# Two sets of seven products without a use, behind the last router product and in front of the part with further rows

## The chip, the cores and the metric

The kernel runs on one core of a Trainium2 chip. The metric is device time in microseconds (us) from the start of the launch to its end. Times of single instructions, waits and granted clocks come from one profiled execution of the kernel before. TensorE is written PE, VectorE DVE, ScalarE ACT, GpSimd POOL and SyncE SP, as the profile writes them.

## What is computed

One layer of an encoder on 2048 tokens (rows) of width 1024: a token mixer, then a hierarchical mixture of experts with a gated embedding per layer.

```python
h1 = layernorm(x)                              # and the mixer: in-projection, conv and pooling groups, out-projection
x1 = layernorm(ALPHA * x + mixer(h1))
g  = softmax(x1 @ w_rg + b_rg); group = argmax(g)              # 4 groups
e  = x1 @ w_re + b_re, only the 8 experts of that group
top2 = top_k(e, 2); weight = softmax(top2) * g[group]
y  = sum over the 2 experts of  weight * ((silu(x1 @ w1) * (x1 @ w3)) @ w2)
ple = sigmoid(x1 @ w_pg + b_pg) * (p @ w_pp)
out = layernorm(ALPHA * x1 + y + ple)
```

Rows are sorted by expert into blocks of 128 slots. A fixed number of slots is planned for each expert; rows beyond that go through a loop over further blocks, whose length is read from the router's result at run time.

## The kernel before

**Products.** Almost every matrix product is made of three products of split operands (`mm3`, L222 to L224): a value is written as a high part (ACT, L356) and the rest (DVE or POOL, L357, `split`), so each weight tile costs one ACT and one DVE or POOL instruction of 128x1024 ahead of its products. A weight comes over SP's DMA queue (L1132) into a raw buffer (RB or RY) and is split into FB. PSUM has eight banks (PS), handed out by `SP = Slots(8)`, the one that has been free longest first; `take` and `get` fetch a bank, `free` gives it back.

**Stages.** First come the mixer's projections for 16 tiles of 128 rows. The out-projection leaves x1 tile by tile; each tile is normalised and turned by PE transposes (`transpose8`, L363). `router(c)` (L883, L884) makes the 36 router logits of the chunk of four tiles c, 16 products of 128x512; `logits` (L890, L891, L898, L899) adds bias, turns and stores them, and `route` (DVE, from L945 on) finds group, two experts and weights of each row. After the last chunk, c = 3, the counts over all rows are made (L1006, L1026, L1024, L1019, L1023 on PE, L1012 to L1070 on DVE), and the slots: DVE builds one-hot tables (L1080, L1082, L1089), PE multiplies them (L1094, 32 products of 128x40 in f32, each of two records in the trace) and the row numbers TBI and TBH (L1099, L1100) start the gathers of the experts' rows (L1387 on POOL's queue).

While that runs, the embedding part works for some of the tiles, PRE (`embed`): products with `w_pg` (L222 to L224), then for each tile L1280 (DVE), a tanh (L1282, ACT), the product with `w_pp`, L1286 and L1290 (DVE), and `base_done` writes the rows to the DRAM tensor `based` (L1321, POOL's queue). Then come the experts, with their first products L1574 and their second ones in `stage2`.

**Where the change touches it.** `run(router(3))` (L1376) makes the last router products; the jobs of the list `bg` are stepped between them. Later, behind the calls of `need` for the first experts' rows, `nc.values_load(novi)` (L1705) reads the number of further blocks on every engine and `tc.For_i` (L1707) loops over them; nothing moves across this loop. The rows of this input need no further block: the trace has no instruction of the loop's body.

**What sets the order.** The text of the program is not the order in which an engine gets its instructions. A scheduler reorders them inside a stretch between branches by its own estimate of times, and PSUM banks and buffers are given out as the program is written. Two instructions are held in order by `add_manual_dep(..., NoSync)`, which adds no wait on the chip. An engine runs its own instructions in the order set, and an instruction that waits holds back those behind it on the same engine.

At L391 and L431 the kernel already has products of the unit matrix `ident` by itself, at its start.

Of the kernel before, what the change touches and what calls it, by code (L numbers as in the profile page):

```python
# [183 lines left out]
def hybrid_conv_pool_hmoe_encoder(ctx, tc, x, p, ln0_g, ln0_b, w_in, b_in, conv_w, pool_w, pool_scale,  # L184
                                  w_o, ln1_g, ln1_b, w_rg, b_rg, w_re, b_re, w1, w3, w2, w_pg, b_pg,
                                  w_pp, ln2_g, ln2_b, out):
    nc = tc.nc
# [10 lines left out]
    PS = psum.tile([128, 8, 512], F32, name="PS")  # L198
    SF, SR, SZ, SP = Slots(NF, NY), Slots(NR), Slots(NZ), Slots(8)
# [30 lines left out]
    ident = consts.tile([128, 128], F32, name="ident")  # L230
# [62 lines left out]
    @contextmanager  # L293
    def behind(last):

        block = nc.cur_bb.bb
        n = len(block.instructions)
        yield
        for ins in list(block.instructions)[n:]:
            if ins.engine in last and ins.engine != mybir.EngineType.SP:  # L300
                tc.add_manual_dep(ins, last[ins.engine].name,
                                  mybir.DependencyInfo(mybir.DependencyClass.NoSync, mybir.DependencyReason.DATA),
                                  reason="in order")

    bg = Background()
    turn = [0]
# [5 lines left out]
    def run(gen):  # L312
        for _ in gen:
            bg.step()
# [8 lines left out]
    def start(name, gen, rate):  # L323
        jobs[name] = gen
        bg.add(gen, rate)

    def need(name):

        if name in jobs:
            gen = jobs.pop(name)  # L330
            n = 0
            while next(gen, DONE) is not DONE:
                n += 1
                if n > 40:
                    bg.step()
            bg.forget(gen)
# [401 lines left out]
    for s, j, c in units:  # L738
# [27 lines left out]
        with behind(beginning if (s, j, c) == (0, 0, 0) else {}):  # L766
            run(unit(s, j, c))
# [60 lines left out]
    def chunk_views(c):  # L828
        h, l = x1T[c]
        return [FB[:, q:q + 4].rearrange("p a (k t) -> p (a k) t", t=CH) for q in (h, l)]  # L830
# [48 lines left out]
    def router(c):  # L879
        vh, vl = chunk_views(c)  # L880
        b = SP.get()
        for k in range(KD):
            nc.tensor.matmul(PS[:, b], wrhv[:, k], vh[:, k], start=k == 0, stop=False)  # L883
            nc.tensor.matmul(PS[:, b], wrlv[:, k], vl[:, k], start=False, stop=k == KD - 1)  # L884
            yield
        start(f"logits{c}", logits(c, b), 1.0)

    def logits(c, b):
        z = SZ.get()
        nc.scalar.activation(ZB[0:36, z, :CH], PS[64:100, b], AF.Identity, bias=brc[0:36])  # L890
        nc.vector.tensor_add(ZB[0:36, z, :CH], ZB[0:36, z, :CH], PS[0:36, b])  # L891
        SP.free(b)
        yield
        yield
        b = SP.get()
        pv = PS[:, b, :4 * 36].rearrange("p (t e) -> p t e", e=36)
        for q in range(4):
            nc.tensor.transpose(pv[:, q], ZB[0:36, z, q * 128:(q + 1) * 128], ident[0:36, 0:36])  # L898
        nc.scalar.copy(LG[:, 4 * c:4 * c + 4], pv)  # L899
        SP.free(b)  # L900
        SZ.free(z)
        yield
# [271 lines left out]
    def take(slots, m=1, align=1):  # L1174
        n = 0
        while not slots.has(m, align):
            bg.step()
            n += 1
            assert n < 10000, "no slot"
        return slots.get(m, align)  # L1180
# [193 lines left out]
    SR.free(g1)  # L1374
    SR.free(b1)
    run(router(3))  # L1376
    SF.free(wrh)
    SF.free(wrl)
    for q in range(3):
# [320 lines left out]
    for m in members[ORDER[0]]:  # L1700
        need(f"g{m}")


    others, bg.jobs = bg.jobs, []
    nov_n = nc.values_load(novi[0:1, 0:1], min_val=0, max_val=NOV)  # L1705
    nc.vector.memset(ctr, 0.0)
    with tc.For_i(0, nov_n, 1) as it:  # L1707
# [5 lines left out]
        b = SP.get()  # L1713
# [146 lines left out]
    def gate_end(z, o, cols):  # L1860
# [3 lines left out]
        return v  # L1864

    def stage(i, t, ahead, behind):

        if i % 2 == 0 and 6 <= i + 4 < len(END):
# [72 lines left out]
    order = [f for fs in plans for part in fs for f in part] + [END[-1]]  # L1941
# [19 lines left out]
def build(nc, arrays):  # L1961
    args = []
    for name in _INS:
        a = arrays[f"in_{name}_dram"]
        args.append(nc.dram_tensor(f"in_{name}_dram", a.shape, mybir.dt.from_np(a.dtype), kind="ExternalInput").ap())
    for i, (shape, dtype) in enumerate(_OUTS):
        args.append(nc.dram_tensor(f"out_{i}_dram", shape, F32, kind="ExternalOutput").ap())
    with tile.TileContext(nc, schedule_with_timeline_sim=True) as tc:
        hybrid_conv_pool_hmoe_encoder(tc, *args)
# [12 lines left out]
```

## Time and profile before

| | us |
|---|---|
| time, median of three executions | 1600.15 |
| lowest and highest | 1597.69, 1601.34 |
| time of the profiled execution | 1601.28 |
| span from its first to its last instruction | 1599.6 |
| PE busy in the span | 1550.9 (97%) |

The profiled execution is one of its own; its time is 1.13 us above the median. The span leaves out 1.7 us around it. In the rows below, PEclk is the clock that PE was granted, 1.00 for 2.4 GHz and 0.50 for 1.2 GHz; in brackets behind a row stands the idle time of the engine just ahead of it and what ended it.

### The profile page before, as it was taken

To read this page: it belongs to the slowest core of one execution; us is meant where nothing else is said; L and a number is where in the kernel's file an instruction comes from. 1 tells how busy PE (TensorE), PEld (TensorE's weight loads), DVE (VectorE), ACT (ScalarE), POOL (GpSimd) and SP (SyncE) were. 2 spreads that over 40 slices of the span, in tenths; PEclk is the share of its full clock that TensorE was granted. 3 is DMA by queue.
4 is the path that set the end of the run, shared out by engine and by line. 5 is a ranking of instruction groups with operands and counts; after the bars stand their busy time and mean duration, and the time that the engine had idled before them with its cause. 6 is when DMAs were issued, how large, how long until landed. Compare 5 with 4: busy or idle time off the path is not lost.

```text
span 1599.6 us, 22570 instructions
## 1 busy us (share of the span) xinstructions
PE 1550.9 (97%) x7837; PEld 1309.8 (82%) x7837; DVE 1169.0 (73%) x1534; ACT 761.2 (48%) x1005; POOL 446.4 (28%) x628
## 2 busy tenths in 40 slices
PE   8999999999999999989999999999999999999994
PEld 7888878887888887778988998888888888878784
DVE  8968574345666767758879878878888777776987
ACT  6332332113111215037878777777787766662221
POOL 3537763441232225110313111111111010005530
PEclk9999999999999999999999999999999999999997
DMA  7546269986385537459798998999999887998971
GB/s 232 196 144 205 67 199 311 342 300 185 112 271 198 171 116 260 132 205 368 282 364 312 406 373 312 370 350 356 356 353 331 312 328 262 388 328 308 363 232 68
DMA packets 205613, 430.64 MB, mean 269 GB/s; under 512 B 19128, under 2 KB 70888, under 8 KB 205496
## 3 DMA queue, kind: packets, MB, share of 16 engines
q1 hardware_dynamic: 161952, 292.06, 51.1%
q0 software_dynamic: 35024, 125.65, 21.5%
q10 hardware_dynamic: 8520, 11.45, 2.1%
q8 instruction: 63, 1.03, 0.3%
q14 instruction: 54, 0.44, 0.1%
HBM read 331.95 MB, written 97.16 MB: 268 GB/s over the span
## 4 chain that ended last, share of the span: by engine, by line
PE 52%; DVE 1%; DMA 1%; ACT 0%; issue 0%; DVEq 0%; ACTq 0%
PE PS L222 12%; PE PS L224 12%; PE PS L223 12%; PE PS L1574 10%; PE PS L363 2%; PE PS L1520 1%; PE PS L1521 1%; PE PS L1644 1%; DMA FB<-x1Td 1%; PE PS L1438 0%; DMA based<-RY 0%; DVE RB L1825 0%; DVE FB L357 0%; ACT FB L356 0%; ACT RY L1686 0%
## 5 line engine op out<-in xcount | busy, mean ns | idle before, releaser
L223 PE MATMUL PS<-FB 128*128 128x512 f32 (+1 forms) x1364 | 527.0, 386 | 6.2 <-DVE FB L357 5.5
L222 PE MATMUL PS<-FB 128*128 128x512 f32 (+1 forms) x1284 | 496.9, 390 | 6.1 <-DVE ZB L1280 2.4
L224 PE MATMUL PS<-FB 128*128 128x512 f32 (+1 forms) x1284 | 494.9, 386 | 2.4 <-DMA FB<-x1Td 2.0
L357 DVE TENSOR_TENSOR FB<-RY,FB 128x1024 fp32r<-128x1024 f32 x243 | 292.4, 1228 | 52.0 <-ACT FB L356 34.7
L223 PEld LDWEIGHTS PS<-FB 128*128 128x128 f32 x1364 | 258.3, 189 | 56.7 <-DVE FB L357 6.5
L222 PEld LDWEIGHTS PS<-FB 128*128 128x128 f32 x1284 | 242.7, 189 | 54.8 <-ACT FB L356 3.5
L224 PEld LDWEIGHTS PS<-FB 128*128 128x128 f32 x1284 | 242.8, 189 | 51.7 <-DMA FB<-x1Td 2.4
L356 ACT CAST FB<-RY 128x1024 fp32r<-128x1024 f32 x247 | 252.5, 1051 | 59.3 <-PE PS L223 20.7
L357 DVE TENSOR_TENSOR FB<-RB,FB 128x1024 fp32r<-128x1024 f32 x197 | 238.4, 1225 | 47.3 <-ACT FB L356 38.5
L356 ACT CAST FB<-RB 128x1024 fp32r<-128x1024 f32 x201 | 207.3, 1051 | 117.5 <-PE PS L223 51.8
L1574 PE MATMUL PS<-FB 128*128 128x296 f32 (+15 forms) x1280 | 174.6, 296 | 3.8 <-issue 3.1
L1574 PEld LDWEIGHTS PS<-FB 128*128 128x128 f32 x1280 | 170.6, 191 | 5.2 <-issue 3.3
L356 ACT CAST FB<-PS 128x1024 fp32r<-128x1024 f32 (+9 forms) x142 | 81.7, 591 | 139.1 <-PE PS L363 83.4
L357 DVE TENSOR_TENSOR FB<-PS,FB 128x1024 fp32r<-128x1024 f32 (+9 forms) x142 | 95.9, 688 | 62.3 <-ACT FB L356 61.8
L223 PE MATMUL PS<-FB,FY 128*128 128x512 f32 x264 | 104.1, 394 | 0.0
L1387 POOL DMA_INDIRECT RY<-x1d,TBI x22 | 45.5, 2070 | 174.2 <-DVE FB L357 132.7
L222 PE MATMUL PS<-FB,FY 128*128 128x512 f32 x216 | 85.7, 397 | 0.0
L224 PE MATMUL PS<-FB,FY 128*128 128x512 f32 x216 | 85.4, 395 | 0.0
L356 ACT CAST FY<-RB 128x1024 fp32r<-128x1024 f32 (+1 forms) x30 | 31.0, 1034 | 110.8 <-PE PS L223 59.7
L1387 POOL DMA_INDIRECT RB<-x1d,TBI x18 | 37.3, 2073 | 153.7 <-DVE FB L357 78.3
L1687 POOL DMA_DIRECT2D yd<-RY x25 | 14.3, 572 | 230.9 <-ACT RY L1686 229.6
L222 PE MATMUL PS<-FY,FB 128*128 128x512 f32 x180 | 71.6, 398 | 0.0
(293 smaller groups left out, 2062.3 us busy)
## 6 DMA issues: line engine op xcount, KB each, us to landing
RY<-in_w_dram SPq DMA_DIRECT2D x233, 512.0 KB, 8.5
RB<-in_w_dram SPq DMA_DIRECT2D x151, 512.0 KB, 9.0
yd<-RB POOLq DMA_DIRECT2D x67, 512.0 KB, 8.0
RB<-in_w_in_dram SPq DMA_DIRECT2D x32, 512.0 KB, 5.7
yd<-RY POOLq DMA_DIRECT2D x25, 512.0 KB, 7.3
RB<-in_x_dram SPq DMA_DIRECT2D x24, 512.0 KB, 4.6
x1Td<-FB POOLq DMA_DIRECT2D x20, 512.0 KB, 6.1
FB<-x1Td SPq DMA_DIRECT2D x20, 512.0 KB, 7.8
```

The source lines that it names most:

```text
L222: nc.tensor.matmul(o, ah, bh, start=start, stop=False)
L223: nc.tensor.matmul(o, ah, bl, start=False, stop=False)
L224: nc.tensor.matmul(o, al, bh, start=False, stop=stop)
L356: nc.scalar.copy(hi, src)
L357: eng.tensor_sub(lo, src, hi)
L363: nc.tensor.transpose(v[:, k], src[:, k * 128:(k + 1) * 128], ident)
L1387: nc.gpsimd.indirect_dma_start(out=RB[0:half or 128, rows[n]], out_offset=None, in_=x1d, in_offset=bass.IndirectOffsetOnAxis(ap=idx, axis=0))
L1520: nc.tensor.matmul(o, xs[0][:, c], wh, start=start, stop=False)
L1521: nc.tensor.matmul(o, xs[0][:, c], wl, start=False, stop=stop)
L1574: nc.tensor.matmul(o, u, v, start=k == 0 and q == 0, stop=k == KD - 1 and q == 1)
L1644: nc.tensor.transpose(v[:, k], g[:, k * 128:(k + 1) * 128], ident[0:m, 0:m])
L1687: nc.gpsimd.dma_start(dst(n), RB[:, q])
```

## The change

A function `unused(n)` takes a PSUM bank, issues n products of the 128x128 unit matrix by itself (f32) into it and frees the bank. Each is held behind the PE instruction ahead of it in the program, the first one behind the last PE instruction issued so far. Nothing reads the result. It is called twice with n = 7: behind `run(router(3))`, and behind the last `need` in front of the loop.

```diff
+    def unused(n):
+
+        pe = [ins for ins in nc.cur_bb.bb.instructions if ins.engine == mybir.EngineType.PE][-1]
+        b = take(SP)
+        for _ in range(n):
+            ins = nc.tensor.matmul(PS[:, b, 128:256], ident, ident, start=True, stop=True).ins
+            tc.add_manual_dep(ins, pe.name,
+                              mybir.DependencyInfo(mybir.DependencyClass.NoSync, mybir.DependencyReason.DATA),
+                              reason="in order")
+            pe = ins
+        SP.free(b)
...
     run(router(3))
+    unused(7)
     SF.free(wrh)
...
     for m in members[ORDER[0]]:
         need(f"g{m}")
+
+    unused(7)
```

The lines of the changed kernel have moved: from L304 on a number is 12 higher, from L1377 on 13, behind the second call 15. So L884 is L896 there, L1094 is L1106, L1280, L1286, L1290 are L1292, L1298, L1302, L357 is L369, and L310 is the product of `unused`.

The first set takes bank 6, the second bank 0. Because banks are handed out in turn, later takers get other banks than before, and the scheduler lays the instructions of all engines out differently from about the last tile's transposes on. Up to there the orders are the same. Three places follow.

PE behind the last router product, before: L884 is the router's last product, L222 to L224 are products of the embedding, L898 turns the logits.

```order
L884 MATMUL PS<-FB 128x512
L223 MATMUL PS<-FB 128x512
L224 MATMUL PS<-FB 128x512
L223 MATMUL PS<-FB 128x512
L224 MATMUL PS<-FB 128x512
L222 MATMUL PS<-FB 128x512
L223 MATMUL PS<-FB 128x512
L224 MATMUL PS<-FB 128x512
L222 MATMUL PS<-FB 128x512
L223 MATMUL PS<-FB 128x512
L224 MATMUL PS<-FB 128x512
L898 MATMUL PS<-ident,ZB 128x36 x4
```

The same place on PE now (L896 is the router's second product, L310 the unused ones, L1018 the row counts that are L1006 before):

```order
L895 MATMUL PS<-FB 128x512
L896 MATMUL PS<-FB 128x512
L895 MATMUL PS<-FB 128x512
L896 MATMUL PS<-FB 128x512
L310 MATMUL PS<-ident 128x128 x7
L1018 LDWEIGHTS RB
L1018 MATMUL PS<-OH,RB 128x32
```

Behind these stand six more of the row counts and then the sixteen embedding products that stood ahead of L884 or between L883 and L884 before; the L223 that came right behind L884 follows them.

PE at the 32 products of the slot tables, before (the first of two groups of 16; between them are 18 embedding products):

```order
L223 MATMUL PS<-FB 128x512
L224 MATMUL PS<-FB 128x512
L1094 MATMUL PS<-RB,RY 128x40 x16
L222 MATMUL PS<-FB 128x512
L223 MATMUL PS<-FB 128x512
```

and now:

```order
L223 MATMUL PS<-FB 128x512
L224 MATMUL PS<-FB 128x512
L1106 MATMUL PS<-RB,RY 128x40 x32
L222 MATMUL PS<-FB 128x512
L223 MATMUL PS<-FB 128x512
```

All 32 stand in one run now, and the embedding products that stood between the groups stand elsewhere.

DVE in front of the loop, before (L357 on PS are parts of gathered rows, L357 on RB a weight):

```order
L357 TENSOR_TENSOR FB<-RB,FB 128x1024
L1286 SCALAR_TENSOR_TENSOR ZB<-ZB,PS 128x512
L357 TENSOR_TENSOR FB<-PS,FB 128x2x128
L357 TENSOR_TENSOR FB<-PS,FB 128x2x64
L1286 SCALAR_TENSOR_TENSOR ZB<-ZB,PS 128x512
L1290 SCALAR_TENSOR_TENSOR RY<-RY,ZB 128x512
L357 TENSOR_TENSOR FB<-PS,FB 128x2x64
L1290 SCALAR_TENSOR_TENSOR RY<-RY,ZB 128x512
L1286 SCALAR_TENSOR_TENSOR ZB<-ZB,PS 128x512
L357 TENSOR_TENSOR FB<-PS,FB 128x2x64
L1290 SCALAR_TENSOR_TENSOR RY<-RY,ZB 128x512
L1286 SCALAR_TENSOR_TENSOR ZB<-ZB,PS 128x512
```

and now, up to the load of the loop's length (L1720):

```order
L369 TENSOR_TENSOR FB<-PS,FB 128x2x64 x3
L369 TENSOR_TENSOR FB<-RY,FB 128x1024 x2
L1292 TENSOR_TENSOR ZB<-PS,RB 128x512 x2
L369 TENSOR_TENSOR FB<-RB,FB 128x1024
L1298 SCALAR_TENSOR_TENSOR ZB<-ZB,PS 128x512 x2
L1302 SCALAR_TENSOR_TENSOR RY<-RY,ZB 128x512 x2
L1298 SCALAR_TENSOR_TENSOR ZB<-ZB,PS 128x512
L1302 SCALAR_TENSOR_TENSOR RY<-RY,ZB 128x512
L1720 TENSOR_LOAD novi
```

The parts of the gathered rows come first now, then two weights that stood further ahead before, and the whole end of the embedding stands behind them.

On PE the second set stands behind the last embedding product and ahead of the sixteen L1574 in front of the loop; before there were twenty, four of them ahead of the last twelve embedding products.

## Rows read from the trace of the kernel before

**Rows 1.** The page: busy time, share of the span and instructions of each engine.

```profile
PE 1550.9 (97%) x7837; PEld 1309.8 (82%) x7837; DVE 1169.0 (73%) x1534; ACT 761.2 (48%) x1005; POOL 446.4 (28%) x628
```

**Rows 2.** Waits of PE, 600 to 740 us: total, times, longest.

```profile
PE PS L223 <- DVE FB L357: 3.2, 1, 3.2
PE PS L1574 <- issue: 3.1, 1, 3.1
PE PS L222 <- DVE ZB L1280: 2.4, 1, 2.4
PE PS L222 <- DVE FB L357: 1.4, 1, 1.4
PE PS L1574 <- DVE ZB L1286: 0.8, 1, 0.8
```

**Rows 3.** Stretches around the last router product: busy time, then PEclk, DMA share, GB/s.

```profile
core 0: us, PE busy (x) PEld busy (x) DVE busy (x) ACT busy (x) POOL busy (x), PEclk, DMA share, GB/s
...
630.03:635.76 5.73, 5.73 (x16) 4.15 (x16) 3.42 (x4) 1.49 (x2) 0.67 (x1) 0.50 0.01 1
...
646.00:649.41 3.41, 3.11 (x7) 2.48 (x8) 2.32 (x16) 0.84 (x2) 0.00 (x0) 0.50 1.00 353
```

**Rows 4.** Timeline there: start, duration, engine, line, operation, [idle ahead].

```profile
625.57 3.32 POOL L357 TENSOR_TENSOR FB<-RY,FB 128x1024 fp32r<-128x1024 f32 x1
...
626.62 3.36 DVE L357 TENSOR_TENSOR FB<-RY,FB 128x1024 fp32r<-128x1024 f32 x1
...
630.03 0.80 PE L223 MATMUL PS<-FB 128*128 128x512 f32 x1 [3.22 <-DVE FB L357]
...
642.80 0.39 PE L224 MATMUL PS<-FB 128*128 128x512 f32 x1
...
643.48 0.39 PE L224 MATMUL PS<-FB 128*128 128x512 f32 x1
...
646.30 0.79 PE L222 MATMUL PS<-FB 128*128 128x512 f32 x1 [2.43 <-DVE ZB L1280]
```

**Rows 5.** Unit products at L431 (ns; starts of the first and last record).

```profile
L431 PE MATMUL PS<-ident x10: 275/275/275, 10.7 to 11.7; 128*128 128x128 f32 x10
```

**Rows 6.** Timeline: splits of transposed rows and a DVE product of the slot tables.

```profile
613.61 1.22 DVE L357 TENSOR_TENSOR FB<-PS,FB 128x1024 fp32r<-128x1024 f32 x1
...
654.58 1.07 ACT L356 CAST FB<-PS 128x512 fp32r<-128x512 f32 x2 [7.28 <-PE PS L1221]
...
655.32 0.67 DVE L357 TENSOR_TENSOR FB<-PS,FB 128x512 fp32r<-128x512 f32 x1
...
678.06 1.23 DVE L1089 TENSOR_TENSOR RY<-POS,io 128x1024 f32<-128x1024 f32 x1 [0.64 <-PE PS L1094]
```

**Rows 7.** Stretches around the slot-table products, columns as in rows 3.

```profile
676.13:680.13 4.00, 4.00 (x35) 3.94 (x34) 3.26 (x5) 1.16 (x2) 0.00 (x0) 1.00 0.02 6
680.13:683.54 3.41, 3.41 (x9) 2.65 (x9) 2.09 (x3) 0.00 (x0) 0.00 (x0) 0.50 0.48 154
...
685.44:689.10 3.66, 3.66 (x34) 3.65 (x33) 0.00 (x0) 0.00 (x0) 0.00 (x0) 1.00 0.18 30
```

**Rows 8.** Timeline in front of the loop.

```profile
712.59 0.50 PE L222 MATMUL PS<-FB 128*128 128x512 f32 x1 [1.35 <-DVE FB L357]
...
713.87 0.39 PE L224 MATMUL PS<-FB 128*128 128x512 f32 x1
714.30 0.69 DVE L1286 SCALAR_TENSOR_TENSOR ZB<-ZB,PS 128x512 f32<-128x512 f32 x1 [1.17 <-PE PS L224]
715.02 0.69 DVE L1290 SCALAR_TENSOR_TENSOR RY<-RY,ZB 128x512 f32<-128x512 f32 x1
...
715.04 2.58 PE L1574 MATMUL PS<-FB 128*128 128x384 f32 x16 [0.78 <-DVE ZB L1286]
...
720.67 4.14 PE L1574 MATMUL PS<-FB 128*128 128x384 f32 x16 [3.05 <-issue]
```

**Rows 9.** Stretch behind the loop, columns as in rows 3.

```profile
721.09:724.50 3.41, 3.41 (x16) 3.41 (x15) 1.85 (x2) 3.40 (x5) 1.92 (x2) 0.50 0.86 280
```

**Rows 10.** The longest wait of PE, 740 to 1600 us: total, times, longest.

```profile
PE PS L224 <- DMA FB<-x1Td: 2.0, 1, 2.0
```

## The prediction

> **What bounds the kernel now.** I read the page first: PE is busy 97% of its span [rows 1], so time can be won only where PE stands still or has a low clock. The waits of PE say where that is near the two places: between 600 and 740 us five waits of 3.2, 3.1, 2.4, 1.4 and 0.8 us, together 10.9 us [rows 2]. Then I laid the granted clock of the stretches over them. PE idles for 3.22 us behind the last router product, and its products then run from 630.03 to 635.76 us at a clock of 0.50; it idles for 2.43 us ahead of 646.30, and the products up to 649.41 are at 0.50 again [rows 3, 4]. At the loop PE stands 0.78 and 3.05 us with sixteen L1574 between, and the products from 721.09 to 724.50 are at half [rows 8, 9]. The fall at 680.13 is another kind: it stands right behind sixteen L1094, with PE busy all of the 4.00 us ahead of it [rows 7]. These are what two sets of unit products can touch: waits, and half clock behind them.
>
> **Why PE stands there.** Behind the router L223 needs a weight whose DVE half ran from 626.62 for 3.36 us. The same form takes 1.22 us at 613.61; at 626.62 POOL was busy with a split of its own, from 625.57 for 3.32 us [rows 4, 6]. At the loop PE has run out of work that may stand in front of it and waits for the end of the embedding.
>
> **The change, part one: the set behind the router.** Ten records of such products start between 10.7 and 11.7 us, 0.111 us apart [rows 5]; seven products are 14 records, 1.56 us. As the order shows, they stand ahead of everything else that PE could do there, so this is on its path whatever the clock does. If nothing else moved, they would lie inside the 3.22 us wait and cost nothing. But the order moved too: sixteen embedding products that stood ahead of the last router products now stand behind the set. Products at full clock start 0.227 us apart (three steps from 642.80 to 643.48 [rows 4]); sixteen make 3.6 us, more than the wait by themselves. So the gap is filled by moved work, with or without the set; and since DVE's split no longer meets POOL's, it comes sooner as well. I take the whole gain: the idle 3.22; half of 5.73 at half clock, 2.87; and, because the router is done about 3 us earlier and DVE's chain of route with it, the idle 2.43 ahead of 646.30 and half of the 3.11 busy us at half clock behind it, 1.56 [rows 3, 4]. Together 10.08. From the other side, if a wait as long as before stood elsewhere in its place, none of it would be left; that bound goes into the range.
>
> Against it stands, first, the set: 1.56. Second, an embedding product now takes the bank of the split that DVE starts at 613.61 and ends at 614.83 [rows 6]. By my count PE gets there near 613.9, an estimate, and waits 0.9 (bounds 0 and 1.2, the whole split).
>
> **What the new order costs between router and loop.** At the counts, the products that stood between the four steps PE, DVE, PE, DVE are moved away, and PE reaches steps that are not ready. I chained the durations by hand. Two of the waits are short DVE steps and half of an ACT pair (0.53 of 1.07), three are DVE halves of 0.67 or L1280 of the same width: 0.7, 0.45, 0.8, 0.2 and 0.9, together 3.05 [rows 6]. Zero is the lower bound, where the scheduler's work ahead of them runs late; 5 times 0.67 + 0.53 = 6.0 is the upper one. I take my chain, as it uses the durations in their order.
>
> At the slot tables the 32 L1094 now follow one another. Each half of the tables needs DVE's L1089, 1.23 us [rows 6]; between the second and the third now stand an L1280, the tanh behind it, L1286 and L1290 (all 512 wide, as L1290 with its 0.69 [rows 8]). So the third table is ready 1.2 + 4 x 0.69 + 1.23 = 5.2 us behind the first, and the sixteen products that cover this take 3.66 [rows 7]: a wait of 1.5. Behind the run PE waits for two short casts of TBI and TBH, since the next product takes the bank: I take 0.5 (bounds 0 and 1.23, one L1089). Together 2.0. Before, the embedding products between the groups covered both.
>
> **The clock at the slot tables.** The trace has sixteen L1094 without a pause, and right behind them the clock at half for 3.41 us with nine products; the second sixteen, from 685.44 at full clock, had no such fall behind them [rows 7]. So this form can bring the clock down though PE is busy. With 32 in one run and a wait of 1.5 us in it I expect one such stretch again, at the same price of 1.7 (half of 3.41): no difference.
>
> The Trainium skill, "TensorE: Matmul & The Clock Gate", section "Why this matters for your kernels", says the opposite of what to fear: the clock falls for gaps in which PE is idle between bursts, so keep those short. By it the run of L1094 would not cost any clock, and the sum would be 1.7 us better. The row at 680.13 speaks against it, as there was no gap; the row at 646.00, behind a gap, agrees with it.
>
> **Part two: the set in front of the loop.** Before, the last embedding product starts at 713.87, L1290 starts at 715.02 and ends 1.45 us behind that product, and PE goes on at 720.67, 5.0 us later, when the rows are in DRAM and the loop is left. In this time PE does only sixteen L1574, 2.58 us [rows 8]. The seven products add 1.56 to 2.58 in a time of 6.4 us: covered, they cost nothing; if that cover went, 1.56. What the loop waits for is DVE. Now two weights' halves, two L1280, a third weight and then six L1286 and L1290 stand at its end: 1.07 for ACT's half that a product releases [rows 6], two weights at 1.22 and eight steps of 0.69, 9.0 us, and with the steps between some 9.4; the product that releases it starts 30 products, 6.8 us, ahead of the last one's end. So L1290 ends 2.6 us behind it instead of 1.45: a loss of 1.15. The wait of 1.35 ahead of 712.59 goes, since the gathered rows' halves stand early on DVE now. Four L1574 that stood in front of the loop stand behind it: 4/16 of 2.58 = 0.65 lost.
>
> The clock: PE has one idle time of some 3.4 us now instead of 0.78 and 3.05. The trace has a fall behind 3.22 and behind 2.43 [rows 3, 4], so I expect it again, at 1.7 as before [rows 9]: no difference.
>
> Behind the loop the experts keep PE full: from 740 us on its longest wait is 2.0 [rows 10], for a load near the end that starts when a product is done, as it still does. The order there is changed in small swaps; what is gained ahead of the loop is kept.
>
> **Sum.** 10.08 - 1.56 - 0.9 - 3.05 - 2.0 + 1.35 - 1.15 - 0.65 = 2.1 us gained. The profiled execution took 1601.28, so it would take 1599.2; the median of 1600.15 becomes 1598.0. A measurement of this kernel tells about 0.2%, 3.2 us, from no change, so this is "within".
>
> **Rivals.**
> 1. The set at the loop does what one would want of it: PE's idle time is short enough behind it that the clock stays at full. That gives 1.7 more: 3.8, 1596.3. For it: the set lies right at the idle time. Against: idle times of 2.43 and 3.22 us both had a fall behind them, and this one is as long.
> 2. No fall at the slot tables, as behind the second group at 689.10: also 1.7 more, 1596.3; with the first, 5.5 and 1594.6. For it: that second group. Against: the first group, and the run is twice as long. The rule of the Trainium skill above would give this time; I give it the chance that the second group does.
> 3. Slower: the clock falls inside the run of L1094. Each product that then runs at half takes up to 0.224 us longer (32 in twice 3.6 us), and the stretch at half may last 6.83 us, as from 628.93 on, not 3.41: 1.7 more. With 16 products at half this costs 3.6 + 1.7 = 5.3, and the time is 3.2 above before: from there on it is slower by over 0.2%. With 20 it is 4.5 + 1.7 = 6.2, 4.1 slower: 1604.2. For it: the fall at 680.13. Against: the trace has no L1094 at half clock, and they may not be bound by the clock at all, in which case the fall is hidden in them.
>
> That the sets do nothing for the gap is part of my forecast: what fills it is the moved products.
>
> **Chances.** My sum, 1598.0, with what lies within 3.2 us: 0.45. Rival 1: 0.14; rival 2: 0.18; both with 0.05 of room for less waiting at the counts: faster 0.37 in all. Rival 3: 0.18. The range reaches from 1594.5, both first rivals, to 1604.0, near the third; beyond lie the longer waits at the counts (6.0 for 3.05) together with a fall in the run, and a gain without those waits.
>
> **What would show it.** Right: PE without a gap over 1 us between the last router product and the counts, and at full clock there; the unit products 0.11 us apart; five short waits at the counts; L1094 in one run of about 9 us with a wait near its middle; one stretch at half behind it and one behind the loop; the end of L1290 2.6 us behind the last embedding product; the loop left about 3 us earlier. Wrong: a gap of 2 us or more ahead of the weight's split behind the router; L1094 over 0.3 us apart; a fall more, or one less, between the router and the experts.

## The result, and the profile after

The changed kernel takes 1609.47 us (median of 9 runs, 1607.12 to 1611.80) where the kernel before took 1601.19 beside it: a ratio of 1.0057, with a 95% interval of 1.0046 to 1.0068. It is 8.3 us slower, where I had forecast 2.1 less. The profiled execution took 1607.12 us (span 1605.5), 5.8 more than that of before, and it is this 5.8 that the rows below can account for. One thing is put right first: the sixteen L1574 (now L1587) that stand ahead of the loop come, in the text, from behind it; the scheduler lifts them, so that something does move across the loop. A stretch in which the granted clock is 0.50 is called a half stretch below.

The page's first part again shows TensorE at 97%; only the engine sums are longer, POOL's by 26 us [rows 1], 24 of them in the gathers (L1400).

```profile
PE 1553.3 (97%) x7864; PEld 1313.7 (82%) x7865; DVE 1174.3 (73%) x1534; ACT 761.7 (47%) x1005; POOL 472.3 (29%) x628
```

The waits of PE from 600 to 740 us have changed their names, but hardly their sum: 11.9 us here, 10.9 for the five of [rows 2].

```profile
PE PS L1587 <- issue: 4.2, 1, 4.2
PE PS L223 <- DVE FB L369: 2.5, 1, 2.5
PE PS L222 <- DVE FB L369: 1.2, 2, 0.8
PE PS L1233 <- issue: 1.0, 1, 1.0
PE PS L222 <- DVE ZB L1292: 0.8, 1, 0.8
PE PS L1035 <- DVE ZB L1033: 0.7, 1, 0.7
PE PS L222 <- ACT FB L368: 0.7, 1, 0.7
PE PS L222 <- DVE TBH L1112: 0.5, 1, 0.5
PE PS L1106 <- DVE RY L1101: 0.3, 1, 0.3
```

The place behind the router, in the timeline. The wait of 3.22 [rows 4] is gone, and the set stands there as 14 records; but three DVE steps of 128x1024, beside POOL's, take some 10 us in a row, and a wait of 2.50 comes 10 us later in its place. (The step that ends this wait is the next DVE split, 1.21 us long from 638.97, which had to come behind them.)

```profile
623.32 1.72 PE L310 MATMUL PS<-ident 128*128 128x128 f32 x14
...
625.90 2.39 POOL L369 TENSOR_TENSOR FB<-RB,FB 128x1024 fp32r<-128x1024 f32 x1 [10.06 <-PE PS L223]
626.08 3.30 DVE L1160 SCALAR_TENSOR_TENSOR FB<-RY,FB 128x1024 fp32r<-128x1024 f32 x1 [0.33 <-ACT FB L1159]
628.97 2.66 POOL L369 TENSOR_TENSOR FB<-RY,FB 128x1024 fp32r<-128x1024 f32 x1 [0.68 <-PE PS L224]
629.30 3.42 DVE L369 TENSOR_TENSOR FB<-RY,FB 128x1024 fp32r<-128x1024 f32 x1
632.47 2.50 POOL L369 TENSOR_TENSOR FB<-RB,FB 128x1024 fp32r<-128x1024 f32 x1 [0.85 <-PE PS L224]
632.64 3.42 DVE L369 TENSOR_TENSOR FB<-RB,FB 128x1024 fp32r<-128x1024 f32 x1
634.93 3.39 POOL L369 TENSOR_TENSOR FB<-RY,FB 128x1024 fp32r<-128x1024 f32 x1
...
640.23 0.80 PE L223 MATMUL PS<-FB 128*128 128x512 f32 x1 [2.50 <-DVE FB L369]
```

The rows show what the two engines do to each other: each of the three DVE steps ends 1.09 us behind the POOL step that was running when it began (POOL's end at 628.29, 631.63 and 634.97, DVE's at 629.38, 632.72 and 636.06), and the POOL step that began while DVE was at work, 634.93, ends 2.26 behind that. So on buffers a step of one engine waits for the running one of the other. The step of before at 626.62 ends 1.09 behind POOL's too [rows 4]. Two more rows of the kernel before bound this: a DVE split that reads a buffer takes 1.22 us where POOL is idle, and the one at 613.61 [rows 6], which reads PSUM, takes 1.22 although POOL has a split from 613.80 on.

```profile
613.80 2.40 POOL L357 TENSOR_TENSOR FB<-RY,FB 128x1024 fp32r<-128x1024 f32 x1 [3.07 <-ACT FB L356]
620.04 1.22 DVE L357 TENSOR_TENSOR FB<-RY,FB 128x1024 fp32r<-128x1024 f32 x1 [0.21 <-PE PS L224]
```

The slot tables, in the same view: DVE ends the first two tables at 676.48, and the second sixteen products take 6.92 us where the first take 3.66 (the sixteen of before took 3.66 too, [rows 7]).

```profile
674.13 2.35 DVE L1101 TENSOR_TENSOR RY<-POS,io 128x1024 f32<-128x1024 f32 x2
...
676.56 3.66 PE L1106 MATMUL PS<-RB,RY 128*128 128x40 f32 x32
680.54 6.92 PE L1106 MATMUL PS<-RB,RY 128*128 128x40 f32 x32 [0.32 <-DVE RY L1101]
687.95 0.79 PE L222 MATMUL PS<-FB 128*128 128x512 f32 x1 [0.49 <-DVE TBH L1112]
```

Stretches: half clock at the wait of 2.50, half clock over the second sixteen and on, and the whole way from 600 us to the first product behind the loop; below it the same for the kernel before.

```profile
core 0: us, PE busy (x), PEclk, DMA share, GB/s
639.69:643.10 3.41, 2.87 (x7) 0.50 0.54 163
680.65:690.89 10.24, 9.75 (x39) 0.50 0.70 231
600.00:724.32 124.32, 112.36 (x556) 0.95 0.53 191
```

```profile
600.00:720.67 120.67, 109.67 (x535) 0.94 0.56 197
```

The loop is left 3.65 us later: 2.69 more of busy time and 0.96 more of idle. In front of it:

```profile
716.07 1.72 PE L310 MATMUL PS<-ident 128*128 128x128 f32 x14
716.64 1.13 POOL L1333 DMA_DIRECT2D based<-RY  x2 [13.92 <-DVE RY L1302]
717.55 2.56 PE L1587 MATMUL PS<-FB 128*128 128x384 f32 x16
717.58 0.69 DVE L1302 SCALAR_TENSOR_TENSOR RY<-RY,ZB 128x512 f32<-128x512 f32 x1
718.56 0.53 POOL L1333 DMA_DIRECT2D based<-RY  x1 [0.79 <-DVE RY L1302]
723.93 1.28 ACT L368 ACT_TABLE_LOAD   x1 [9.59 <-DMA based<-RY]
```

Three writes of rows now start within 1.9 us of each other, and from the last one's start to ScalarE's next work 5.37 us go by; before it was 4.27. That the writes land later because they come so close together is likely, but not shown.

```profile
716.01 0.53 POOL L1321 DMA_DIRECT2D based<-RY  x1 [2.05 <-DVE RY L1290]
720.28 1.28 ACT L356 ACT_TABLE_LOAD   x1 [8.85 <-DMA based<-RY]
```

Behind the loop two waits are new or longer than those of before (2.0 for x1Td, [rows 10], none at L1657):

```profile
PE PS L224 <- DMA FB<-x1Td: 3.2, 2, 2.6
PE PS L1657 <- DVE ZB L1649: 1.5, 1, 1.5
```

Compared step by step on VectorE and ScalarE, the changed kernel is 3.65 us later where the loop is left, 4.7 from 740 to 1000 us, 6.3 behind the wait at L1657 (1268.78), 5.95 from 1450 to 1490 us and 5.94 at the end. So the wait at L1657 counts. The longer wait for x1Td does not: it is made up near the end, where the kernel before had a half stretch (3.41 us at 1512.98) that is not there now.

### The profile page after: what moved, and what is told of

The parts are those of the page before. It is cut to its first block, busy times and chain, and to the rows that moved or that the text cites. A ratio compares the mean times of both kernels' runs of the same rounds, so it can differ in the third digit from the quotient of the medians.

```text
span 1605.5 us, 22633 instructions
## 1 busy us (share of the span) xinstructions
PE 1553.3 (97%) x7864; PEld 1313.7 (82%) x7865; DVE 1174.3 (73%) x1534; ACT 761.7 (47%) x1005; POOL 472.3 (29%) x628
## 4 chain that ended last, share of the span: by engine, by line
PE 51%; DMA 1%; DVE 1%; ACT 1%; issue 0%; DVEq 0%; ACTq 0%
PE PS L222 12%; PE PS L224 12%; PE PS L223 12%; PE PS L1587 10%; PE PS L375 2%; PE PS L1533 1%; PE PS L1534 1%; DMA FB<-x1Td 1%; PE PS L1657 1%; DVE FB L369 0%; PE PS L1451 0%; DMA based<-RY 0%; ACT FB L368 0%; ACT RY L1699 0%; DVE RB L1840 0%
## 5 line engine op out<-in xcount | busy, mean ns | idle before, releaser
L223 PE MATMUL PS<-FB 128*128 128x512 f32 (+1 forms) x1364 | 525.0, 385 | 4.6 <-DVE FB L369 3.9
L222 PE MATMUL PS<-FB 128*128 128x512 f32 (+1 forms) x1284 | 497.3, 388 | 6.1 <-ACT FB L368 3.0
L224 PE MATMUL PS<-FB 128*128 128x512 f32 (+1 forms) x1284 | 492.3, 385 | 4.2 <-DMA FB<-x1Td 3.2
L369 DVE TENSOR_TENSOR FB<-RY,FB 128x1024 fp32r<-128x1024 f32 x243 | 292.8, 1230 | 57.7 <-ACT FB L368 34.8
L223 PEld LDWEIGHTS PS<-FB 128*128 128x128 f32 x1364 | 257.2, 189 | 54.3 <-DVE FB L369 4.5
L222 PEld LDWEIGHTS PS<-FB 128*128 128x128 f32 x1284 | 242.0, 189 | 55.7 <-ACT FB L368 4.5
L224 PEld LDWEIGHTS PS<-FB 128*128 128x128 f32 x1284 | 241.9, 188 | 53.2 <-DMA FB<-x1Td 4.1
L369 DVE TENSOR_TENSOR FB<-RB,FB 128x1024 fp32r<-128x1024 f32 x197 | 240.2, 1235 | 52.5 <-ACT FB L368 41.7
L1587 PE MATMUL PS<-FB 128*128 128x336 f32 (+15 forms) x1280 | 174.3, 296 | 4.2 <-issue 4.2
L1587 PEld LDWEIGHTS PS<-FB 128*128 128x128 f32 x1280 | 170.5, 191 | 5.1 <-issue 4.5
L368 ACT CAST FB<-PS 128x1024 fp32r<-128x1024 f32 (+10 forms) x142 | 81.6, 593 | 145.7 <-PE PS L375 86.9
L369 DVE TENSOR_TENSOR FB<-PS,FB 128x1024 fp32r<-128x1024 f32 (+10 forms) x142 | 96.1, 690 | 62.0 <-ACT FB L368 59.6
L1400 POOL DMA_INDIRECT RY<-x1d,TBI x22 | 69.6, 3163 | 225.9 <-DVE FB L369 165.9
L223 PE MATMUL PS<-FB,FY 128*128 128x512 f32 x264 | 104.1, 394 | 0.0
L222 PE MATMUL PS<-FB,FY 128*128 128x512 f32 x216 | 85.7, 397 | 0.0
L224 PE MATMUL PS<-FB,FY 128*128 128x512 f32 x216 | 85.4, 395 | 0.0
L1400 POOL DMA_INDIRECT RB<-x1d,TBI x18 | 39.6, 2201 | 155.0 <-DVE FB L369 91.9
L222 PE MATMUL PS<-FY,FB 128*128 128x512 f32 x180 | 71.6, 398 | 0.0
L224 PE MATMUL PS<-FY,FB 128*128 128x512 f32 x180 | 70.8, 394 | 0.0
```

Source lines behind the costliest of these rows:

```text
L222: nc.tensor.matmul(o, ah, bh, start=start, stop=False)
L223: nc.tensor.matmul(o, ah, bl, start=False, stop=False)
L224: nc.tensor.matmul(o, al, bh, start=False, stop=stop)
L368: nc.scalar.copy(hi, src)
L369: eng.tensor_sub(lo, src, hi)
L1400: nc.gpsimd.indirect_dma_start(out=RB[0:half or 128, rows[n]], out_offset=None, in_=x1d, in_offset=bass.IndirectOffsetOnAxis(ap=idx, axis=0))
```

## The experiments

Two theories were open. **The products**: twice 14 records, some 3.1 us more work on TensorE's path. **The order**: the bank that each set takes and gives back, which changes the banks of all later takers and with them the scheduler's order. Line numbers shift by a few from kernel to kernel; where it matters, the line of the kernel before is named beside a row.

**Which part of the change it is.** First the banks taken and freed, and no products; the second kernel has the products, but puts the bank back at its old place in the row of free ones:

```diff
-        for _ in range(n):
-            ins = nc.tensor.matmul(PS[:, b, 128:256], ident, ident, start=True, stop=True).ins
-            ...
         SP.free(b)
```

> Both places still take a PSUM bank and give it back, but issue no product. The order of the other instructions stays that of the changed kernel but for some twenty rows of PE, the 32 products of the slot tables still in one run. Theory A (the order that follows from the banks costs the time, through the slot tables at half clock): still slower than before by 5 to 9 us, and the second sixteen slot-table products near 6.9 us instead of 3.7; against the changed kernel at most the 1.56 us of the first set better. Rival B (the products themselves cost it): level with before, within 2 us, and the tables at 3.7.

Measured: 1608.74 (ratio 1.0051, 1.0034 to 1.0068): the loss is there without a product. The second sixteen of the slot tables take 7.02 us there, at half clock.

```diff
+        age = dict(SP.age)
         b = take(SP)
 ...
-        SP.free(b)
+        SP.age[b] = age[b]
```

> Both sets are issued, but the bank goes back to its place in the row of free banks, so that later takers get the banks they had before. The slot tables stand in two groups of sixteen again. Theory A: no loss; the waits at the counts and at the tables are those of before, the place behind the router gains a part of its 3.2 us wait and of its half clock, so 0 to 5 us faster than before, 1596 to 1601. Rival B (the products cost it): slower than before by 5 us or more here too.

Measured: 1600.17 (ratio 0.9998, 0.9986 to 1.0010): both sets, and no loss. What the set gives behind the router is in part taken back by a longer wait for the step that was 2.43 us late in [rows 4] (L1280, here L1294):

```profile
PE PS L222 <- DVE ZB L1294: 4.0, 1, 4.0
```

Then each set by itself, with its bank taken as in the change:

> Only the set in front of the loop, with its bank handed on as in the change; the order up to the last embedding products is that of before, so that the wait and the half clock behind the router and the two groups of slot-table products are those of before. Theory A: up to 715 us nothing changes. If the seven products keep the clock up behind the loop, the stretch at half behind 721 us goes and 1.7 us are won; if not, no change: 1599 to 1601.5. What comes behind the loop is ordered anew, which can cost or bring 1 to 2 us. Rival B: each set costs time where it stands, here about 4 us.

> The changed kernel without its second set: only the set behind the router, with its bank taken as in the change. Theory: it is the bank that the first set takes that turns the order of all that follows it; the loss is all there, 1606.5 to 1610.5. Rival: the loss needs the second set as well, which stands between the last embedding product and the sixteen L1587 while the loop waits for the based rows: without it 1602 to 1605.

The second alone: 1600.65 (0.9997, 0.9986 to 1.0008). The first alone: 1610.05 (1.0059, 1.0038 to 1.0080). So it is the first set, and of it the bank. The waits of PE in the kernel with the banks alone are those of the changed kernel, the first two even longer:

```profile
PE PS L1587 <- issue: 6.9, 1, 6.9
PE PS L223 <- DVE FB L1160: 3.6, 1, 3.6
```

**The products in the old order.** Here and in the next kernels the order on every engine is written out by hand (each instruction chained to the one before it on its engine, as the kernel's own helpers do), so that nothing moves but what is named.

```diff
+    def unused(n, b):
+        for _ in range(n):
+            nc.tensor.matmul(PS[:, b, 128:256], ident, ident, start=True, stop=True)
 ...
     run(router(3))
+    unused(7, 2)
 ...
         need(f"g{m}")
+    unused(7, 2)
```

> The order of the kernel before on every engine, kept by hand, and the two sets of seven at the two places of the change, in a bank that nothing waits for. Theory: the products by themselves neither win nor lose, since each set lies in an idle time that ends when DVE is done: 14 records 0.111 us apart lie in the wait of 3.22 behind the router; at the loop they run over the 0.78 and the sixteen L1574 start 0.8 later, which the wait of 3.05 behind them takes in. 1599.5 to 1602. If the set kept the clock behind the router, up to 2.9 us would be won there, but the wait at L1280 of 2.43 would take most of it back, as where both sets took their bank and put it back: 1598.5. Rival: the products are what costs: 1.56 us for each set or more, 1603 to 1605.

Measured: 1601.51 (0.9995, 0.9983 to 1.0008): the products neither win nor lose. The timeline shows the set inside the wait, 1.62 of which is left, at full clock behind it; and the wait at L1280 (here L1285) longer than its 2.43 before:

```profile
626.59 1.72 PE L308 MATMUL PS<-ident 128*128 128x128 f32 x14
629.93 0.50 PE L223 MATMUL PS<-FB 128*128 128x512 f32 x1 [1.62 <-DVE FB L362]
...
644.14 0.54 PE L222 MATMUL PS<-FB 128*128 128x512 f32 x1 [2.88 <-DVE ZB L1285]
```

**The run of 32 products.** In the order of the kernel before, only TensorE's 18 embedding products between the two groups of L1094 were put behind the second group; there are no sets.

```diff
-PE: L1094 x16, embedding x18, L1094 x16
+PE: L1094 x16, L1094 x16, embedding x18
```

> The order of the kernel before on every engine, with no unused products; only TensorE's 18 embedding products that stand between the two groups of sixteen L1094 stand behind the second group now, so that the 32 follow one another. Theory (rival 3 of the prediction, which the changed kernel seems to show): the clock falls inside the run, the second sixteen take some 6.9 us as in the changed kernel instead of 3.66, and half clock goes on behind the run; with up to 0.8 us of waits, 3 to 6 us slower than before, 1604 to 1607. Rival (what I predicted): one half stretch behind the run and none in it, as before, at most 1.5 us of waits: 1600.5 to 1602.5. If so, the fall in the changed kernel comes from something else of its order.

Measured: 1603.45 (1.0014, 1.0002 to 1.0026), between what the two theories gave. The interval is wide, but the trace is plain: the run is one row without a wait, the clock is at half from 4.06 us after its start, for 10.24 us, and everything behind it starts 3.4 us later than in the kernel before (the loop is left at 724.04, not 720.67). The fall itself is not new: in the kernel before it comes at 680.13, 3.99 us after the first sixteen began, and lasts 3.41 [rows 7]. New is that sixteen more L1094 follow at once, that the clock stays at half for 10.24, and that they run in it.

```profile
676.25 10.01 PE L1094 MATMUL PS<-RB,RY 128*128 128x40 f32 x64
```

```profile
680.31:690.55 10.24, 10.24 (x40) 0.50 0.73 260
```

If the run is the fault, breaking it up in the changed kernel should cure it. With 9, then with all 18 of the last embedding products ahead of it put between the groups:

```diff
-PE: embedding x9, L1106 x16, L1106 x16
+PE: L1106 x16, embedding x9, L1106 x16
```

> The order of the changed kernel with both sets, except that 9 of the 18 embedding products ahead of the slot tables stand between their two groups of sixteen. Theory: the run of 32 is what brings the clock down there; broken up, the second sixteen take some 3.7 us instead of 6.9, and the half stretch of 10.24 us is one of 3.4 or none: 3 to 5 us faster than the changed kernel, 1604.5 to 1606.5. Rival: the clock falls there because of what stands ahead of the tables; then it stays at 1609.5 within 1.

> The order of the changed kernel with both sets, but with all 18 embedding products that stand last ahead of the slot tables between their two groups of sixteen, as many as in the kernel before. Theory: in the changed kernel those products also cover the making of the first table on VectorE (L1101 ends near 675.3 us), so TensorE waits 2 to 3 us ahead of the first sixteen, and the clock falls behind that wait as it did with 9 between; the second sixteen stay at full: 1606.5 to 1609.5, next to nothing won. Rival: the run alone is what costs; broken up as before it is cured, 3 to 4 us faster than the changed kernel: 1605 to 1606.5.

With 9: 1608.54 (1.0044, 1.0028 to 1.0060), no cure. With 18: 1612.36 (1.0076, 1.0059 to 1.0092), worse by 3 and above what I expected. The tables in the timelines of the two:

```profile
674.73 4.82 PE L1106 MATMUL PS<-RB,RY 128*128 128x40 f32 x32 [0.75 <-DVE RY L1101]
...
683.33 4.01 PE L1106 MATMUL PS<-RB,RY 128*128 128x40 f32 x32
```

```profile
678.79 5.37 PE L1106 MATMUL PS<-RB,RY 128*128 128x40 f32 x32 [2.76 <-DVE RY L1101]
...
689.80 3.66 PE L1106 MATMUL PS<-RB,RY 128*128 128x40 f32 x32
```

TensorE now reaches the tables before DVE has made the first one, so each product that is moved between the groups is missing ahead of the first. With 9 there, the clock falls in the first group instead of the second: half stretches of 6.83 (from 677.21 us) and 3.41 (from 687.45), together as long as the one of the changed kernel. With 18, TensorE stands still for 2.76, the clock falls behind that (6.83 from 680.66) and the second sixteen are at full, as I expected. Not all of the 3 us belongs to the tables, though: the profile of this kernel has a half stretch of 10.24 us from 653.35, ahead of the first moved product, where the order is that of the changed kernel and the changed kernel has none. That breaking up the run cures the loss, as I expected with 9, is refuted; with DVE as late as it is, the cost only takes another form. In the kernel before the first two tables were ready at 675.43, with 18 products still in hand:

```profile
672.01 3.42 DVE L1089 TENSOR_TENSOR RY<-POS,io 128x1024 f32<-128x1024 f32 x2
```

In the changed kernel they are ready at 676.48, though the last router product starts 3.3 us earlier (623.1 for 626.42). From that product to the tables DVE needs 4.4 us more. Its meetings with POOL can account for some 3.6 of them, an estimate from the rows: three steps of 3.3 to 3.4 us and a small one of 1.70 (L980) now, one of 3.36 and a small one of 2.38 (L946) before. No run takes just these meetings away, so this cause is argued, not shown; the kernel with both sets and the old banks has such meetings too (DVE steps of 3.21 and 2.24) and does not lose.

**Filling the idle times themselves.** If these products hold the clock, larger sets in the old order, each as long as the idle time it lies in, should pay: 14 behind the router, 14 ahead of the wait for L1280, and at the loop 3 ahead of and 13 (then 5) behind the sixteen L1574; then the first two sets without the loop's, and the loop's 13 without the others. The edit is the one above, with other numbers.

> The order of the kernel before on every engine, kept by hand, and unused products in all four idle times of TensorE: 14 behind the router (3.1 of 3.22 us), 14 ahead of the wait for L1280 (3.1 us, the wait was 2.43 and grows if the clock holds ahead of it), 3 ahead of the sixteen L1574 (0.67 of 0.78) and 13 behind them (2.9 of 3.05). Theory (idle time brings the clock down at these three places): the half stretches at 628.9, 646.0 and 721.1 us are gone, and 1.5 to 4.5 us are won, 1596.5 to 1599.5. Rival 1: such products don't hold the clock, it falls as before: 1600.5 to 1602. Rival 2: DVE and the DMAs set the times at these places anyway, so that a kept clock only makes the next wait longer: clock kept, waits longer, 1600 to 1601.5.

> As the kernel with all four idle times filled, but with 5 products instead of 13 behind the sixteen L1574 (1.1 us of the wait of 3.05). Theory: in the kernel with 13, TensorE was the last to come to the loop, 717.35 us, let the other engines go and started again 5.3 us later, while in the kernel before it starts 0.39 us behind ScalarE's table load. With 5 it is not the last any more, and starts within 0.5 us of ScalarE, some 3 us earlier than before: 1596.5 to 1599. Rival: what keeps TensorE behind the loop is its next weights, whose load starts when the loop is left; then it goes on at about the same time as with 13, 1602 to 1604.

> The order of the kernel before, 14 unused products behind the router and 14 ahead of the wait for L1280, none at the loop. Theory: the half stretches at 628.9 and 646.0 us are gone, TensorE comes to the loop some 3 us earlier and stays that much ahead; at the loop 0.78, sixteen L1574, 3.05 and half clock as before: 1597 to 1599.5. Rival: what is won ahead of the loop is lost behind it, as with 13 products behind the sixteen: 1600.5 to 1603.

> The order of the kernel before and nothing but 13 unused products behind the sixteen L1574 in front of the loop, 2.9 us in a wait of 3.05. Theory: if TensorE ends them after the other engines have come to the loop, it starts again some 5 us later, so 3 to 5 us are lost: 1603 to 1605.5; its half stretch behind the loop may go (1.7 won): then 1602 to 1604. Rival: they lie in the wait and cost nothing, clock kept: 1598.5 to 1600.5.

Measured: with all four 1603.75 (1.0018, 1.0007 to 1.0029); with 5 behind the sixteen 1602.25 (1.0009, 0.9997 to 1.0020); without the loop's 1600.70 (1.0000, 0.9988 to 1.0011); the loop's 13 alone 1600.64 (1.0006, 0.9994 to 1.0017). No theory had its time: none of the four is faster, and the loop's 13 alone cost nothing. In the first three kernels, though, the clock part came out: the clock is 1.00 over both old idle times ahead of the loop. In the kernel without the loop's sets TensorE is busy throughout, at full clock, over both of them (columns as in [rows 3]), and it leaves the loop at 717.07, 3.6 us earlier than before:

```profile
626.00:646.00 20.00, 20.00 (x120) 17.33 (x119) 18.79 (x46) 6.71 (x11) 9.19 (x5) 1.00 0.41 133
```

Compared step by step, 3.1 us of this are kept up to 1450 us; the profiled span is only 1.2 us shorter, and the medians are the same. The rest goes where waits for x1Td (3.2 in all, 2.0 before) and a half stretch (at 1482.56, before at 1512.98) stand near the end, and these differ from run to run: with the two sets alone in the old order the waits come to 4.5. At the loop, the two kernels with sets at all four places arrive some 3 us early and lose it at once. With 5 products TensorE ends them at 715.64, before the other engines go on, and still starts 3.87 us after ScalarE; with none there, 0.45 after it:

```profile
717.18 1.28 ACT L361 ACT_TABLE_LOAD   x1 [8.84 <-DMA based<-RY]
...
721.05 17.02 PE L1581 MATMUL PS<-FB 128*128 128x384 f32 x96 [5.42 <-DVE FB L362]
```

```profile
716.62 1.28 ACT L361 ACT_TABLE_LOAD   x1 [8.84 <-DMA based<-RY]
717.07 0.53 PE L1581 MATMUL PS<-FB 128*128 128x384 f32 x2 [3.15 <-issue]
```

Being last at the loop is thus not the whole reason: with 5 it is not last, and late all the same. Nor is the weight's split that the row names: in the second kernel, of the same order, TensorE starts ahead of those splits (718.99). Why it is late there stays open. It has no part in the changed kernel, where TensorE starts 0.39 behind ScalarE, as before.

## Why the prediction was wrong

The forecast had the change within 0.2%; it is 0.57% slower and beyond the range, whose upper end was 1604.0. By its own terms, in us of the profiled executions:

| term | forecast | measured |
|---|---|---|
| waits 3.22 and 2.43 and the half clock behind them | +10.08 | +6.15: a wait of 2.50 and half clock (1.43) at 640.23 took part of their place |
| set behind the router | -1.56 | -1.56 |
| wait for a DVE split ahead of it | -0.9 | -0.80 |
| five waits at the counts | -3.05 | -3.57 |
| waits at the slot tables | -2.0 | -0.81 |
| clock at the slot tables | 0 | -3.0: second sixteen +3.26, behind them 1.47 where it was 1.70 |
| wait ahead of 712.59 gone | +1.35 | +1.35 |
| end of the embedding | -1.15 | -1.7: L1290 0.6, the landing of its rows 1.1 |
| four L1574 behind the loop | -0.65 | -0.65 |
| clock behind the loop | 0 | 0 (one half stretch of 3.41 again, at 725.03) |
| behind the loop, the four L1574 left out | 0 | -1.6: 1.5 of it at L1657 |
| sum | +2.1 | -6.2 (the two executions differ by 5.8) |

Of the 8.3 us between forecast and sum, 3.9 are in the first row, 3.0 in the clock at the tables and 1.6 behind the loop; the others nearly cancel.

**The step that failed first** is "since DVE's split no longer meets POOL's, it comes sooner as well. I take the whole gain". The order showed embedding products filling the gap, and they do: TensorE has no wait over 1 us from 614 to 637 us. But as those products end they let POOL go on (two of its rows name L224 as releaser, one L223), and POOL and DVE split weights at the same time again: DVE's step at 626.62, 3.36 us long [rows 4], was replaced by three, 3.30, 3.42 and 3.42, not by one of 1.22. The term of 10.08 came to 6.15. My price for the step without POOL was read from a wrong row: the split at 613.61 is not "the same form", as it reads PSUM, and POOL was at work beside it; the right row, 620.04, has the same 1.22. I had named the bound ("if a wait as long as before stood elsewhere in its place") and then left the sum at the other end. The row for the price was there; I did not lay POOL's splits beside DVE's in the new order.

**The second** is "The clock at the slot tables ... no difference". Rival 3, which I gave 0.18, is what happened: sixteen products at half, estimated at 3.6 us longer, measured 3.26. In each of the four kernels with the 32 in one run and a trace of it the second sixteen run at half in whole or in part (6.92 us in the changed one, 7.02 with the banks alone, 5.18 with the first set alone, some 6.4 in the old order); where 18 products stand between, the second sixteen take 3.66. The kernel of before with nothing changed but this run loses 3.4 us by its trace. My reason against it, that these products might not be bound by the clock, is refuted. But the rival too had only part of the cause: broken up in the changed kernel, the run costs as much, as DVE is late there.

**The third** is "what is gained ahead of the loop is kept". 1.6 went behind it, most of it in the wait at L1657. The "small swaps" are not free: this wait stands in each kernel in which a set hands its bank on, the one with the second set alone too, and in none of the others.

**What was right**: the sets themselves cost next to nothing and do next to nothing (shown by the sets in the old order, and by both sets with the banks kept); what fills the gap is the moved products (with the banks alone there is no gap either, from the router's last product to 631 us); of the terms not named above each came within 0.6 of its forecast, except the waits at the tables, where TensorE came 1.2 us behind the first table and so waited less; the loop's clock did not change. The Trainium skill's rule ("TensorE: Matmul & The Clock Gate", section "Why this matters for your kernels"), that idle gaps bring the clock down, agrees with the two filled gaps, where the clock stayed at 1.00. It does not say that nothing else does, and I had read it so: the run of 32 fell to 0.50 without a gap.

The profiled execution of the changed kernel was the quickest of its nine, so of the 8.3 us between the medians some 2.5 are not in the rows. Its mean granted clock is 0.989, that of the median execution 0.987 and of the two slowest 0.985; 0.002 of 1607 us is 3.2 us, an estimate of the most that this can cost, so more half clock is enough to explain them, in stretches that no trace shows. One order need not give one pattern of clock: in the kernel with 13 products at the loop, whose order ahead of it is that of before, the half stretch behind the router was 3.41 us long, not 6.83, and there was none at 646, behind a wait of 2.75. That kernel's last write of rows starts at 713.74, 2.27 us earlier than before, with no other cause in the order.

## What to carry to other kernels

An instruction that takes a buffer from a rotating pool changes the buffers of everything behind it, and with them what a scheduler may put where; try such a filler with the buffer given back at its old place before its own effect is judged. When a change sends more work ahead of a wait, look at what that work releases on the other engines: a gap that is filled is worth what the next late engine leaves of it. And a run of small products is a cost of its own if the clock can fall inside it, but breaking it up pays only with work that is not needed to cover a wait elsewhere.

## What the runs showed of the hardware

- TensorE's clock fell with no idle time at all: 4.06 us into an unbroken run of 128x40 f32 products (row of the one run above). These products follow the clock: sixteen take 3.66 us at full and 6.92 at half.
- Products of a unit matrix, 0.12 us a record, filled two idle times (28 records in 3.29 us each) in three kernels, and the clock stayed at 1.00 in all three. Without them, in four traces of the same order, it fell behind the first idle time in all four and behind the second in three.
- A DVE step of 128x1024 on buffers took 1.21 to 1.23 us alone, and 3.30 to 3.42 where it met one of POOL's: it ended 1.09 behind that. POOL's took 2.39 to 2.66 where it came first, and 3.39 where it had to wait for DVE's. A DVE step that read PSUM took 1.22 beside one of POOL's.
- With unused products directly ahead of the loop's load, TensorE started again 4.99 (13 and 3 products), 3.87 (5 and 3) and 1.82 us (13 alone) after ScalarE; in the other kernels 0.39 to 0.48, but 1.68 in the one with both sets and the old banks. Why is not known.
